# Small parameters as rows, squares shared in another order, and x turned two channel tiles at a time

## The chip, the cores and the metric

The kernel runs on one core of a Trainium2 chip. The core has a matrix engine (TensorE, PE in the profile; its weight loads are PEld), a vector engine (VectorE, DVE), a scalar engine (ScalarE, ACT), GpSimd (POOL) and a queue that starts transfers (SyncE, SP). Matrix products read SBUF, the on-chip memory of 128 partitions, and write PSUM, eight banks of 128 x 512 numbers in 32 bits. The metric is the device time of one execution in microseconds (us). The kernel before takes 730.1 us, the median of three runs (729.89 to 731.35).

## The reference

One layer of a diffusion backbone on x (512 tokens, 1024 channels), with 256 context tokens and a conditioning vector c:

```python
sh, sc, gt = split(silu(c) @ w_mod + b_mod, 3)
h = rmsnorm(x, pre_g) * (1 + sc) + sh            # and the same for the context, with c_ctx
parts = split_in(h @ w_in)                       # 10 parts of 1024 columns
q, k, v = rope(parts[4]), rope(parts[5]), parts[6]
attn = neighbourhood_attention(q, k, v, k_ctx, v_ctx, rpb)     # window 8 x 16, and all context keys
y_a = (silu(z_a) * b_gate * dwconv3(c_gate * x_in, conv_w, conv_b)) @ w_out_conv
y_b = (silu(z_b) * attn) @ w_out_attn
y = (sigmoid(g_a) * y_a + sigmoid(g_b) * y_b) @ w_o
out = x + gt * rmsnorm(y, post_g)
```

Everything is in 32-bit floating point. The change concerns the first two lines and the beginning of the third.

## The kernel before

The kernel keeps activations with channels on partitions and tokens along the free axis, in eight tiles of 128 channels (`KT` = 8). A product of near 32-bit precision is made of three products in the reduced type fp32r: each operand is split into a high part (a cast on ACT, L70) and a low part (a subtraction on DVE, L71), and high x high, high x low and low x high are added in PSUM.

The first 52 us are written in a fixed order for PE, DVE, ACT and SP (`tc.manual_schedule`, L313): on each engine the instructions stand as the program issues them. Behind it a scheduler orders the work, from its own costs.

The fixed part does the following.

1. SP loads the vector c (`crow`, L314), the four token tiles of x (`xn`, `load_x`, 128 tokens x 1024 channels each, L315), the small parameters (`sp`, L316: gains, biases and convolution weights, 72 columns), and then for each channel tile k two slabs of w_mod (`wm`, `load_slab`, L249) and one piece of the first three weight chunks (`fraw`, `load_first`, L284). All of these stand in one queue.
2. PE spreads silu(c) over all partitions (`spread`, L353, two products of one row); ACT copies the two halves into `cb` (`kept`, L357).
3. For each token tile i, `square(i)` takes the sum of squares (L333 on DVE or L337 on ACT), `root(i)` its root on ACT (L341), and `norm(i)` the reciprocal on DVE (L345) and the scaling of x: on DVE for tiles 0 to 2 (L347), on ACT for tile 3 (L349).
4. `condition(k, 0, [0])` and `condition(k, 0, [1])` make the scale and the shift of channel tile k, each a sum over 1024 products on DVE (L259). The first uses `bsc1`, a copy of a part of `sp` plus one (L375). L393 multiplies the scale by the gain.
5. PE turns x (a transpose by a product with the identity): the channel tiles 0 and 1 of all four token tiles first (L386), with products that only keep PE busy in between (`keep_busy`, L362, 128 x 256 with a result that is not used). Each such product and each spread counts as two in the profile.
6. For k = 0 to 7: ACT casts the weights (`cast_first`, L289), DVE makes the low part (`rest_first`, L293), ACT modulates the turned tile with scale and shift (L398) and casts it (L70), DVE makes its low part (L71). Then `steps(k)` makes 18 products of 128 x 512 into the six accumulators `acc` (L305, L306, L309), and behind them `turn_x(k + 2)` turns the tile that is two further (L298, four transposes). Turned tiles alternate between two PSUM banks (`tps`).

Behind this part come the convolution branch, the attention with its keys, queries and values, the gates, the merge and the output projection. PE works there almost without a gap.

Of the kernel before, what the change touches and what calls it, by code (L numbers as in the profile page):

```python
# [9 lines left out]
F32 = mybir.dt.float32  # L10
# [5 lines left out]
P = 128  # L16
# [11 lines left out]
def layer(ctx: ExitStack, tc, xp, ctxt, ctxT, cc, wmod, small, wfirst, win, wout, wo, rel, tab, out):  # L28
# [204 lines left out]
    with ExitStack() as p0:  # L233
# [3 lines left out]
        def load_x(src, i, n, tag, pool, bufs=1):  # L237
            xt = pool.tile([P, D], F32, name=n, tag=tag, bufs=bufs)
            nc.sync.dma_start(xt, src[i * P:(i + 1) * P])
            return xt  # L240
# [50 lines left out]
        def rest_first(k):  # L291
            H, L = first[k]
            nc.vector.tensor_sub(L, raws[k], H.bitcast(F32))  # L293
# [7 lines left out]
        def steps(k):  # L301
            H, L = first.pop(k)
            for i in range(6):
                cs = slice(i * P, (i + 1) * P)
                nc.tensor.matmul(acc[i], lhsT=H[:, cs], rhs=hx[0][k], start=k == 0, stop=False)  # L305
                nc.tensor.matmul(acc[i], lhsT=L[:, cs], rhs=hx[0][k], start=False, stop=False)  # L306
            for i in range(6):
                cs = slice(i * P, (i + 1) * P)
                nc.tensor.matmul(acc[i], lhsT=H[:, cs], rhs=hx[1][k], start=False, stop=k == KT - 1)  # L309
# [2 lines left out]
        E = mybir.EngineType  # L312
        with tc.manual_schedule(engines={E.PE, E.DVE, E.Activation, E.SP}):  # L313
            nc.sync.dma_start(crow, cc[0:1].rearrange("o (a n) -> o a n", a=2))  # L314
            xn = [load_x(xp, i, f"x{i}", f"u{i}", hp) for i in range(4)]  # L315
            nc.sync.dma_start(sp, small)  # L316
            for k in range(3):
                load_slab(k)
                load_first(k)

            nc.vector.memset(eps, EPS)
            nc.vector.memset(ones, 1.0)
            nc.vector.memset(allones, 1.0)

            nc.scalar.activation(crow, crow, AF.Silu)
            nc.scalar.activation(const.tile([P, 1], F32, name="dummy"), eps, AF.Sqrt)
            junk_a = hp.tile([P, D], F32, name="junka", tag="a1")

            def square(i):
                top = tops[:, i:i + 1]  # L330
                if i < 2:
                    junk = st.tile([P, D], F32, name="junk")
                    nc.vector.tensor_tensor_reduce(  # L333
                        out=junk, in0=xn[i], in1=xn[i], scale=1.0, scalar=0.0, op0=ALU.mult, op1=ALU.add, accum_out=top
                    )
                else:
                    nc.scalar.activation(junk_a, xn[i], AF.Square, accum_out=top)  # L337

            def root(i):
                top = tops[:, i:i + 1]  # L340
                nc.scalar.activation(top, top, AF.Sqrt, bias=eps, scale=1.0 / D)  # L341

            def norm(i):
                top = tops[:, i:i + 1]
                nc.vector.reciprocal(top, top)  # L345
                if i < 3:
                    nc.vector.tensor_scalar(out=xn[i], in0=xn[i], scalar1=top, scalar2=None, op0=ALU.mult)  # L347
                else:
                    nc.scalar.mul(xn[i], xn[i], top)  # L349

            def spread(i):
                ps = tps()
                nc.tensor.matmul(ps, lhsT=ones, rhs=crow[:, i], start=True, stop=True)  # L353
                return ps

            def kept(i, ps):
                nc.scalar.copy(cb[:, 0, i * S:(i + 1) * S], ps)  # L357

            def keep_busy(n):

                for _ in range(n):
                    nc.tensor.matmul(acc[5][:, :256], lhsT=ident, rhs=cb[:, 0, :256], start=True, stop=True)  # L362

            wide = [spread(i) for i in range(2)]
            square(0)
            square(1)
            kept(0, wide[0])
            root(0)
            norm(0)
            root(1)  # L370
            norm(1)
            kept(1, wide[1])
            square(2)
            root(2)
            nc.vector.tensor_scalar(out=bsc1, in0=sp[:, BM + 8:BM + 16], scalar1=1.0, scalar2=None, op0=ALU.add)  # L375
            nc.vector.tensor_scalar(out=hcv, in0=sp[:, CW:CW + 32], scalar1=0.5, scalar2=None, op0=ALU.mult)
            norm(2)
            square(3)
            root(3)
            condition(0, 0, [0])  # L380
            norm(3)
            turned_x = {k: tps() for k in range(2)}
            for t in range(4):
                keep_busy(1 if t < 2 else 2)
                for k in range(2):
                    nc.tensor.transpose(turned_x[k][:, t * P:(t + 1) * P], xn[t][:, k * P:(k + 1) * P], ident)  # L386
            keep_busy(3)

            for k in range(KT):
                cast_first(k)  # L390
                condition(k, 0, [1])
                col = cols.pop((k, 0))
                nc.vector.tensor_mul(col[:, 0:1], col[:, 0:1], sp[:, PG + k:PG + k + 1])  # L393
                rest_first(k)
                if k + 1 < KT:
                    condition(k + 1, 0, [0])
                m = st.tile([P, S], F32, name="m", bufs=2)
                nc.scalar.activation(m, turned_x.pop(k), AF.Identity, bias=col[:, 1:2], scale=col[:, 0:1])  # L398
                split(hx[0][k], hx[1][k], m)
                if k + 3 < KT:  # L400
                    load_slab(k + 3)
                    load_first(k + 3)
                elif k == 5:
                    after = Chunk(order[3])
                steps(k)
                if k + 2 < KT:
                    turned_x[k + 2] = turn_x(k + 2)
            chunk.ahead[3] = after.split()
            nc.sync.dma_start(cb[:, 1], cc[1:2].broadcast_to([P, D]))
            nc.scalar.activation(cb[:, 1], cb[:, 1], AF.Silu)  # L410
            cn = [load_x(ctxt, i, f"c{i}", f"a{2 + i}", hp) for i in range(2)]
            ctT4 = [hp.tile([P, 4, C], F32, name=f"ctT{i}", tag="a0" if i == 0 else "u3") for i in range(2)]
            for i in range(2):
                nc.sync.dma_start(ctT4[i], ctxT[:, 4 * i:4 * i + 4])
            for i in range(2):
                nc.scalar.activation(junk_a, cn[i], AF.Square, accum_out=topc[:, i:i + 1])
            nc.scalar.activation(topc, topc, AF.Sqrt, bias=eps, scale=1.0 / D)
            nc.vector.reciprocal(topc, topc)

            for i in range(2):  # L420
                nc.vector.tensor_scalar(out=diag[:, i], in0=ident, scalar1=topc[:, i:i + 1], scalar2=None, op0=ALU.mult)
# [454 lines left out]
```

## Time and profile before

| | |
|---|---|
| median of three runs | 730.1 us |
| the profiled execution | 730.62 us |
| its span, first to last instruction | 728.8 us |
| PE busy | 718.0 us (99%) |
| DVE, ACT busy | 515.1 us (71%), 331.9 us (46%) |
| step 0 begins on PE (L305) | 15.88 us |
| step 1 begins on PE | 20.52 us |

The span is counted from the first instruction; the device time has about 1.8 us around it. In the timeline a row gives the start, the length, the engine with its line, the tiles that are written and read, how often rows were joined, and in brackets how long the engine had stood idle and what released it. The length of an instruction contains its start-up and its drain, so that the next one on the same engine may start before the end that is shown.

### The profile page before, as it was taken

The numbers are of one execution on the slowest core, as the hardware profiler recorded it, in microseconds if no ns is written. First come the engines' busy times: TensorE is split into PE (matmuls) and PEld (weight loads), VectorE is DVE, ScalarE is ACT, GpSimd is POOL, SyncE is SP. The second block draws the span as 40 slices with busy tenths as digits, with TensorE's granted clock in tenths as the row PEclk, the third lists the DMA queues.
The fourth block names the chain that finished last, engine by engine and source line by source line (L and its number), as shares of the span: only waits on it lengthen the run. The fifth ranks groups of instructions, "written<-read, shape, count | busy, mean of one in ns | idle before, by whom it ended". The sixth has DMA issues, their size and how long they took to land.

```text
span 728.8 us, 9358 instructions
## 1 busy us (share of the span) xinstructions
PE 718.0 (99%) x3512; PEld 602.5 (83%) x3512; DVE 515.1 (71%) x1060; ACT 331.9 (46%) x619; POOL 0.7 (0%) x6
## 2 busy tenths in 40 slices
PE   7999999999999999999999999999999999999996
PEld 4888888888888888888888888888888888888885
DVE  6979999996998968879879779675844324335323
ACT  6565533663564654655536446434823213314221
POOL 0000000000000000000000000000000000000000
PEclk9999999999999999999999999999999999999999
DMA  8985873213212222121322212222133233235402
GB/s 334 405 310 176 317 268 125 92 65 105 65 66 73 70 76 73 58 86 59 116 73 73 73 58 73 96 78 73 58 115 102 72 116 103 71 116 177 169 10 107
DMA packets 25967, 86.63 MB, mean 119 GB/s; under 512 B 3009, under 2 KB 3393, under 8 KB 25922
## 3 DMA queue, kind: packets, MB, share of 16 engines
q1 hardware_dynamic: 25778, 85.84, 33.8%
q8 instruction: 27, 0.44, 0.2%
q10 hardware_dynamic: 144, 0.20, 0.1%
q14 instruction: 18, 0.15, 0.1%
HBM read 83.93 MB, written 2.10 MB: 118 GB/s over the span
## 4 chain that ended last, share of the span: by engine, by line
PE 95%; DVE 1%; DMA 1%; ACT 1%; SPq 0%; issue 0%; DVEq 0%; ACTq 0%
PE ps L117 20%; PE ps L116 20%; PE ps L115 20%; PE ps L128 6%; PE ps L752 6%; PE ps L597 4%; PE ps L581 4%; PE ps L132 3%; PE ps L549 3%; PE ps L140 2%; PE ps L305 2%; PE ps L309 2%; PE ps L306 2%; DMA wm<-in_wmod 1%; PE ps L558 1%; PE ps L144 1%
## 5 line engine op out<-in xcount | busy, mean ns | idle before, releaser
L115 PE MATMUL ps<-h,w 128*128 128x512 f32 x528 | 207.4, 393 | 0.0
L117 PE MATMUL ps<-h,w 128*128 128x512 f32 x528 | 206.0, 390 | 0.0
L116 PE MATMUL ps<-h,w 128*128 128x512 f32 x528 | 205.7, 390 | 0.0
L71 DVE TENSOR_TENSOR w<-raw,w 128x1024 fp32r<-128x1024 f32 (+1 forms) x98 | 113.1, 1173 | 59.0 <-ACT w L70 58.8
L70 ACT CAST w<-raw 128x1024 fp32r<-128x1024 f32 (+1 forms) x98 | 96.9, 1016 | 94.2 <-PE ps L117 64.6
L117 PEld LDWEIGHTS ps<-h,w 128*128 128x128 f32 x528 | 99.1, 188 | 20.8
L116 PEld LDWEIGHTS ps<-h,w 128*128 128x128 f32 x528 | 99.2, 188 | 20.3
L115 PEld LDWEIGHTS ps<-h,w 128*128 128x128 f32 x528 | 99.1, 188 | 20.2
L572 ACT ACTIVATE pt<-ps,m 128x512 f32<-128x512 f32 x64 | 44.3, 693 | 59.0 <-DVE m L569 59.0
L565 DVE CUSTOM_DVE_ANT_1 ps<-ps,bt 128x512 f32<-128x512 f32 x56 | 38.6, 700 | 15.1 <-PE ps L549 12.0
L71 DVE TENSOR_TENSOR TL<-ps,TH 128x512 fp32r<-128x512 f32 x64 | 42.7, 680 | 5.2 <-ACT TH L70 5.2
L128 PE MATMUL ps<-w,h 128*128 128x512 f32 x128 | 45.2, 395 | 0.0
L712 DVE SCALAR_TENSOR_TENSOR g<-g,ps 128x512 f32<-128x512 f32 x16 | 11.0, 687 | 42.5 <-PE ps L117 42.5
L70 ACT CAST TH<-ps 128x512 fp32r<-128x512 f32 x64 | 35.0, 588 | 6.6 <-PE ps L581 6.4
L630 ACT ACTIVATE g<-ps 128x512 f32<-128x512 f32 x16 | 9.6, 598 | 59.6 <-PE ps L117 59.6
L132 PE MATMUL ps<-w,h 128*128 128x256 f32 x128 | 36.0, 281 | 0.0
L581 PE MATMUL ps<-ident,pt 128*128 128x128 f32 x256 | 33.3, 272 | 0.0
L574 DVE TENSOR_SCALAR pt<-pt,z 128x512 f32<-128x512 f32 x64 | 30.8, 482 | 1.0
L581 PEld LDWEIGHTS ps<-ident,pt 128*128 128x128 f32 x256 | 29.4, 140 | 2.2
L597 PE MATMUL ps<-TH,V 128*128 128x256 f32 (+1 forms) x96 | 28.5, 319 | 0.0
L128 PEld LDWEIGHTS ps<-w,h 128*128 128x128 f32 x128 | 24.0, 187 | 5.3
L597 PE MATMUL ps<-TL,V 128*128 128x256 f32 (+1 forms) x96 | 27.7, 319 | 0.0
(158 smaller groups left out, 1183.5 us busy)
## 6 DMA issues: line engine op xcount, KB each, us to landing
raw<-in_win SPq DMA_DIRECT2D x74, 512.0 KB, 4.2
wm<-in_wmod SPq DMA_DIRECT2D x34, 512.0 KB, 6.9
raw<-in_wout SPq DMA_DIRECT2D x16, 512.0 KB, 3.9
bt<-in_rel SPq DMA_DIRECT2D x16, 256.0 KB, 2.6
raw<-in_wo SPq DMA_DIRECT2D x8, 512.0 KB, 3.7
fraw<-in_wfirst SPq DMA_DIRECT2D x8, 384.0 KB, 8.3
x<-in_xp SPq DMA_DIRECT2D x4, 512.0 KB, 5.3
xr<-in_xp SPq DMA_DIRECT2D x4, 512.0 KB, 6.2
```

Source lines behind the costliest of these rows:

```text
L70: nc.scalar.copy(H, src)
L71: nc.vector.tensor_sub(L, src, H.bitcast(F32))
L115: nc.tensor.matmul(ps, lhsT=H[:, k, cs], rhs=mH[k], start=k == 0, stop=False)
L116: nc.tensor.matmul(ps, lhsT=H[:, k, cs], rhs=mL[k], start=False, stop=False)
L117: nc.tensor.matmul(ps, lhsT=L[:, k, cs], rhs=mH[k], start=False, stop=k == KT - 1)
L128: nc.tensor.matmul(ps, lhsT=mH[k][:, ts], rhs=both[:, k].rearrange("p a c -> p (a c)"), start=k == 0, stop=False, skip_group_check=True,)
L132: nc.tensor.matmul(ps[:, :256], lhsT=mL[k][:, ts], rhs=H[:, k], start=False, stop=k == KT - 1, skip_group_check=True)
L565: nc.vector.tensor_tensor_reduce(out=s3, in0=s3, in1=bt[:, e::4 - e][:, 0:2], scale=1.0, scalar=-3.0e38, op0=ALU.add, op1=ALU.max, accum_o ...
L572: nc.scalar.activation(pt, s, AF.Exp, bias=m, scale=1.0, accum_out=z)
L581: nc.tensor.transpose(tp[:, c], pt[:, c * P:(c + 1) * P], ident)
L597: nc.tensor.matmul(o3[:, dst], lhsT=V[p][:, kt, h], rhs=src(t), start=n == 0 and t is TH, stop=n == len(work) - 1 and t is TL,)
L752: nc.tensor.matmul(ps, lhsT=mm[m][k][:, ts], rhs=w[k][:, cols], start=k + o == 0, stop=k == KT - 1 and o == 2)
```

## The change

There are three edits, all in the fixed part. The kernel's lines behind them move by four to seven numbers.

- The host passes the small parameters as 72 rows of 128 numbers in place of 128 rows of 72. They are loaded as `rows`, third in SP's queue, ahead of x2 and x3 rather than behind them. PE turns them into a PSUM bank behind the two spreads, and ACT copies the result to `sp`.
- DVE takes the squares of tiles 0 and 2, ACT those of 1 and 3 (before: DVE 0 and 1, ACT 2 and 3). The second `kept` comes ahead of the second square, and `norm(3)` ahead of the first condition sum. The small `hcv` instruction moves into the loop, behind `rest_first(0)`.
- `turn_x(k + 2)` no longer follows each step. In steps 1, 3 and 5, after six of the 18 products, two tiles are turned one after the other.

```diff
@@ steps(k)
             for i in range(6):
+                if i == 3 and k % 2 and k + 2 < KT:
+
+                    for n in (k + 1, k + 2):
+                        turned_x[n] = turn_x(n)
                 cs = slice(i * P, (i + 1) * P)
                 nc.tensor.matmul(acc[i], lhsT=H[:, cs], rhs=hx[0][k], start=k == 0, stop=False)
                 nc.tensor.matmul(acc[i], lhsT=L[:, cs], rhs=hx[0][k], start=False, stop=False)
@@ the fixed part
             nc.sync.dma_start(crow, cc[0:1].rearrange("o (a n) -> o a n", a=2))
-            xn = [load_x(xp, i, f"x{i}", f"u{i}", hp) for i in range(4)]
-            nc.sync.dma_start(sp, small)
+            xn = [load_x(xp, i, f"x{i}", f"u{i}", hp) for i in range(2)]
+            rows = st.tile([72, P], F32, name="rows")
+            nc.sync.dma_start(rows, small)
+            xn += [load_x(xp, i, f"x{i}", f"u{i}", hp) for i in range(2, 4)]
...
             def square(i):
                 top = tops[:, i:i + 1]
-                if i < 2:
+                if i % 2 == 0:
...
             wide = [spread(i) for i in range(2)]
+            nc.tensor.transpose(acc[0][:, :72], rows, ident[:72, :72])
             square(0)
-            square(1)
             kept(0, wide[0])
             root(0)
             norm(0)
+            kept(1, wide[1])
+            nc.scalar.copy(sp, acc[0][:, :72])
+            square(1)
+            square(2)
             root(1)
+            root(2)
             norm(1)
-            kept(1, wide[1])
-            square(2)
-            root(2)
             nc.vector.tensor_scalar(out=bsc1, in0=sp[:, BM + 8:BM + 16], scalar1=1.0, scalar2=None, op0=ALU.add)
-            nc.vector.tensor_scalar(out=hcv, in0=sp[:, CW:CW + 32], scalar1=0.5, scalar2=None, op0=ALU.mult)
             norm(2)
             square(3)
             root(3)
+            norm(3)
             condition(0, 0, [0])
-            norm(3)
...
                 rest_first(k)
+                if k == 0:
+                    nc.vector.tensor_scalar(out=hcv, in0=sp[:, CW:CW + 32], scalar1=0.5, scalar2=None, op0=ALU.mult)
...
                 steps(k)
-                if k + 2 < KT:
-                    turned_x[k + 2] = turn_x(k + 2)
@@ the host
     def cols(z):
-        return z.reshape(-1, 128).T
+        return z.reshape(-1, 128)
```

On DVE, in the lead-in, the row of names is: `x_120`, `x_122` and so on are the token tiles 0, 1, 2, 3 in order (in the changed kernel `x_126` is tile 2 and `x_128` tile 3), `ISA` with `junk,tops` is a square, `ISA` with `junk,col` a condition sum. Before:

```order
L345 RECIPROCAL tops<-tops 128x1 [waits Activation_49]
L347 TENSOR_SCALAR x_122<-x_122,tops 128x1024 [waits DVE_49]
L375 TENSOR_SCALAR bsc_102<-sp 128x8 [waits DMAHW5_49]
L376 TENSOR_SCALAR hcv<-sp 128x32
L345 RECIPROCAL tops<-tops 128x1 [waits Activation_49]
L347 TENSOR_SCALAR x_124<-x_124,tops 128x1024 [waits DMAHW3_49,DVE_49]
L259 ISA junk,col_178<-wm,cb,bsc_102 128x1024 [waits DMAHW6_49]
L259 ISA col_178 128x1
L345 RECIPROCAL tops<-tops 128x1 [waits Activation_49]
L259 ISA junk,col_178<-wm,cb,sp 128x1024 [waits DMAHW7_49,DVE_49]
```

And now, at the same place:

```order
L339 ISA junk,tops<-x_126 128x1024 [waits DMAHW4_49]
L339 ISA tops 128x1
L351 RECIPROCAL tops<-tops 128x1 [waits Activation_49]
L353 TENSOR_SCALAR x_122<-x_122,tops 128x1024 [waits DMAHW2_49,DVE_49]
L383 TENSOR_SCALAR bsc_102<-sp 128x8
L351 RECIPROCAL tops<-tops 128x1 [waits Activation_49]
L353 TENSOR_SCALAR x_126<-x_126,tops 128x1024 [waits DVE_49]
L351 RECIPROCAL tops<-tops 128x1 [waits Activation_49]
L259 ISA junk,col_182<-wm,cb,bsc_102 128x1024 [waits DMAHW6_49]
L259 ISA col_182 128x1
L259 ISA junk,col_182<-wm,cb,sp 128x1024 [waits DMAHW7_49,DVE_49]
```

The square of tile 2, which waits for that tile's load, stands ahead of the scaling of tile 1, and the reciprocal of tile 3 ahead of both condition sums.

On PE, the lead-in's keep-busy products and turns (`ident,x`) before:

```order
L353 MATMUL ps<-crow,ones 128x512
L362 MATMUL ps<-cb,ident 128x256 [waits Activation_49,Pool_49]
L386 MATMUL ps<-ident,x_120 128x128 [waits DVE_49]
L386 MATMUL ps<-ident,x_120 128x128 [waits Activation_49]
L362 MATMUL ps<-cb,ident 128x256
L386 MATMUL ps<-ident,x_122 128x128 [waits DVE_49]
L386 MATMUL ps<-ident,x_122 128x128
L362 MATMUL ps<-cb,ident 128x256 x2
```

And now:

```order
L359 MATMUL ps<-crow,ones 128x512
L371 MATMUL ps<-ident,rows 128x72 [waits DMAHW3_49,Pool_49]
L368 MATMUL ps<-cb,ident 128x256 [waits Activation_49]
L393 MATMUL ps<-ident,x_120 128x128 [waits DVE_49]
L393 MATMUL ps<-ident,x_120 128x128 [waits Activation_49]
L368 MATMUL ps<-cb,ident 128x256
L393 MATMUL ps<-ident,x_122 128x128 [waits DVE_49]
L393 MATMUL ps<-ident,x_122 128x128
L368 MATMUL ps<-cb,ident 128x256 x2
```

The order of turns and keep-busy products is the same; the turn of the 72 rows stands ahead of them, and what each turn waits for on DVE and ACT comes at another time.

At the end of step 0 PE had the turn of a tile ahead of step 1 (`h_81` is the modulated tile of step 1):

```order
L309 MATMUL ps<-h_80,fH 128x512 x5
L298 MATMUL ps<-ident,x_120 128x128 [waits PE_49]
L298 MATMUL ps<-ident,x_122 128x128
L298 MATMUL ps<-ident,x_124 128x128
L298 MATMUL ps<-ident,x_126 128x128
L305 MATMUL ps<-h_81,fH 128x512 [waits Activation_49]
L306 MATMUL ps<-h_81,fL 128x512 [waits DVE_49]
```

Now step 1 follows at once and has two turns inside (the first is shown):

```order
L313 MATMUL ps<-h_80,fH 128x512 x5
L309 MATMUL ps<-h_81,fH 128x512 [waits Activation_49]
L310 MATMUL ps<-h_81,fL 128x512 [waits DVE_49]
L309 MATMUL ps<-h_81,fH 128x512
L310 MATMUL ps<-h_81,fL 128x512
L309 MATMUL ps<-h_81,fH 128x512
L310 MATMUL ps<-h_81,fL 128x512
L298 MATMUL ps<-ident,x_120 128x128 [waits PE_49]
L298 MATMUL ps<-ident,x_122 128x128
L298 MATMUL ps<-ident,x_126 128x128
L298 MATMUL ps<-ident,x_128 128x128
```

Eight transposes stand behind the first six products of step 1, and nothing between the last product of step 0 and the first of step 1.

More of the change, by code (lines that the diff above doesn't have):

```diff
@@ L827, in cols @@
     def cols(z):
-        return z.reshape(-1, 128).T
+        return z.reshape(-1, 128)
     small = np.ascontiguousarray(np.concatenate(
         [cols(a["pre_g"][0]), cols(a["post_g"][0]), cols(a["b_mod"][0])]
-        + [cols(a["conv_w"][0][i]) for i in range(3)] + [cols(a["conv_b"][0])], axis=1))
+        + [cols(a["conv_w"][0][i]) for i in range(3)] + [cols(a["conv_b"][0])]))
     xp = np.ascontiguousarray(a["x"][0].reshape(ROWS, COLS, 1024).transpose(1, 0, 2)).reshape(512, 1024)
```

## The prediction

> **What bounds the kernel now.** I read the page's busy times and its chain of waits first, then the list of who waited for whom on TensorE (PE), then the timeline of the first 25 us.
>
> ```profile
> PE 718.0 (99%) x3512; PEld 602.5 (83%) x3512; DVE 515.1 (71%) x1060; ACT 331.9 (46%) x619; POOL 0.7 (0%) x6
> ...
> PE 95%; DVE 1%; DMA 1%; ACT 1%; SPq 0%; issue 0%; DVEq 0%; ACTq 0%
> ...
> PE ps L386 <- ACT x L349: 0.6, 1, 0.6
> PE ps L549 <- ACT pt L572: 0.4, 1, 0.4
> PE ps L305 <- ACT h L70: 0.3, 1, 0.3
> ```
>
> PE is the bound: 99% busy, 95% of the chain. Its waits after the opening vector are three short ones, two of them before its first real product at L305. So the change, which touches only the first 50 us, can move the end in two ways: by moving the start of step 0 (L305 of `steps(0)`), or by putting a gap into PE's work behind it. A microsecond lost or won there is one in the total.
>
> The timeline of the lead-in shows what the start of step 0 hangs on.
>
> ```profile
> 5.76 1.22 DVE L333 CUSTOM_DVE_ANT_0 junk<-x 128x1024 f32<-128x1024 f32 x1
> 5.86 0.30 ACT L341 ACTIVATE tops<-tops,eps 128x1 f32<-128x1 f32 x1
> 6.91 0.16 DVE L345 RECIPROCAL tops<-tops 128x1 f32<-128x1 f32 x1
> 7.23 0.56 ACT L357 COPY cb<-ps 128x512 f32<-128x512 f32 x1
> 7.77 0.16 DVE L345 RECIPROCAL tops<-tops 128x1 f32<-128x1 f32 x1
> 7.96 0.75 DVE L347 TENSOR_SCALAR x<-x,tops 128x1024 f32<-128x1024 f32 x1
> 8.50 1.06 ACT L337 ACTIVATE junka<-x 128x1024 f32<-128x1024 f32 x1 [0.70 <-DMA x<-in_xp]
> 9.68 0.29 ACT L341 ACTIVATE tops<-tops,eps 128x1 f32<-128x1 f32 x1
> 9.88 1.04 ACT L337 ACTIVATE junka<-x 128x1024 f32<-128x1024 f32 x1
> 10.01 0.17 DVE L375 TENSOR_SCALAR bsc<-sp 128x8 f32<-128x8 f32 x1 [1.30 <-DMA sp<-in_small]
> 10.09 0.18 DVE L376 TENSOR_SCALAR hcv<-sp 128x32 f32<-128x32 f32 x1
> 11.05 0.29 ACT L341 ACTIVATE tops<-tops,eps 128x1 f32<-128x1 f32 x1
> 11.22 1.28 DVE L259 CUSTOM_DVE_ANT_0 junk<-wm,cb,bsc 128x1024 f32<-128x1024 f32 x1
> 12.43 0.16 DVE L345 RECIPROCAL tops<-tops 128x1 f32<-128x1 f32 x1
> 12.61 1.28 DVE L259 CUSTOM_DVE_ANT_0 junk<-wm,cb,sp 128x1024 f32<-128x1024 f32 x1
> 12.62 1.15 ACT L349 ACTIVATE x<-x,tops 128x1024 f32<-128x1024 f32 x1 [1.28 <-DVE tops L345]
> 13.68 0.82 ACT L289 CAST fH<-fraw 128x768 fp32r<-128x768 f32 x1
> 13.82 0.15 DVE L393 TENSOR_TENSOR col<-col,sp 128x1 f32<-128x1 f32 x1
> 14.40 0.77 ACT L398 ACTIVATE m<-ps,col 128x512 f32<-128x512 f32 x1
> 15.88 0.51 PE L305 MATMUL ps<-h,fH 128*128 128x512 f32 x1 [0.31 <-ACT h L70]
> ```
>
> Three things are to be seen. x2 came at 8.50, late against x1 (whose square began at 5.76). The wait for `sp` at 10.01 looks like the target, but the first condition sum behind it (11.22) waits for its own slab. And the modulation at 14.40 follows the cast on ScalarE (ACT), not DVE, whose column was made at 13.82.
>
> **The change, part by part.** *Small parameters as rows.* The transfer stands third instead of fifth in SP's queue, so x2 and x3 wait behind it and the slabs do not. Its price: x3 was in use at 9.88 and `sp`, queued behind it, at 10.01, so 0 to 0.3 us; I take 0.15. x2 is then usable at 8.65, x3 at 10.03 or before. PE's turn of 72 rows stands behind the two spreads, in time that PE does not need. The copy out of PSUM on ACT lies between the 0.30 us of a 128x1 and the 0.56 us of a 128x512 row: 0.3 us, behind the second `kept`, which cannot start before 7.05 (the end of the spreads, below). Queued behind the copy is the square of x1.
>
> *Squares.* ACT now squares x1 from about 8.0, and its root starts 1.18 us later (8.50 to 9.68), done by 9.5. DVE squares x2 from 8.65 and takes the reciprocal of x1 1.15 us later (5.76 to 6.91), at 9.80. Reciprocal and scaling take 0.86 us to the next instruction (6.91 to 7.77): `bsc1` at 10.66, 0.08 later (10.01 to 10.09) x2's reciprocal at 10.74, x3's at 11.60. On ACT the root of x2 starts at about 9.92, the square of x3 0.20 later (9.68 to 9.88), its root 1.17 after that (9.88 to 11.05) at 11.29, done 11.58: just in time. Then the two condition sums. `norm(3)` now stands ahead of the first, so this sum waits for x3's whole chain: it starts 0.19 after 11.60, at 11.79, not at 11.22. The second follows 1.3 us later and the column 1.21 us after that (12.61 to 13.82), at 14.33.
>
> ACT is eased: it scales x3 at 11.8 instead of 12.62. But `fH` needs its load, for which the row says only that it had come by 13.68, so the cast frees ACT by 14.40 at the latest. The column reaches ACT 0.25 us after its start (rows below, 18.41 to 18.66), so the modulation starts at 14.58 instead of 14.40. From there to step 0 it is 1.48 us as before (14.40 to 15.88): **16.06, that is +0.18**.
>
> *Turns.* The rows around the end of step 0:
>
> ```profile
> 18.41 0.15 DVE L393 TENSOR_TENSOR col<-col,sp 128x1 f32<-128x1 f32 x1
> 18.66 0.78 ACT L398 ACTIVATE m<-ps,col 128x512 f32<-128x512 f32 x1 [0.81 <-DVE col L393]
> 18.77 1.56 PE L309 MATMUL ps<-h,fH 128*128 128x512 f32 x6
> 19.47 0.62 ACT L70 CAST h<-m 128x512 fp32r<-128x512 f32 x1
> 20.16 0.60 PE L298 MATMUL ps<-ident,x 128*128 128x128 f32 x4
> 24.78 0.60 PE L298 MATMUL ps<-ident,x 128*128 128x128 f32 x4
> ```
>
> A step with its turn takes 24.78 - 20.16 = 4.62 us. In the row of six, the starts of products are (1.56 - 0.39)/5 = 0.23 us apart, so 18 products are 4.18 and four turns 0.44. Six tiles turned one by one or in pairs are 24 instructions either way: 2.64 us, no difference. What is lost is a cover: the turn behind step 0 hid that `h` of step 1 is ready only at 19.47 + 0.62 = 20.09, made at DVE's pace. DVE's work behind the column stays as dense (the `hcv` instruction of 0.09 us moves to between 15.3 and 15.4, where DVE had stood idle before), so 20.09 stays. PE leaves step 0 at 16.06 + 4.18 = 20.24, so the uncovered wait costs nothing; but it means that a start before 15.9 would no longer be worth anything. Later turns end before the modulation that reads them is due: tile 2 by about 22.1 against 22.6. Tiles 4 and 6 come out some 1 to 1.5 us later than before, within step 3 and 5, but their `h` still stands more than 1 us ahead of its step. Cost nothing; if that lead were gone, about 1 us each.
>
> Behind step 7 the order is a scheduler's, and it comes out nearly as before: on PE one small product moves back by three, on ACT and DVE some neighbours change places until about 125 us. PE waits there for 0.4 us in all (L549, above), so the loads and casts have room to shift; cost nothing.
>
> *PE's lead-in.* This is the part that is easily missed. Between the turns of x stand products that only keep PE busy (L362).
>
> ```profile
> 3.27 3.78 PE L353 MATMUL ps<-crow,ones 1*128 1x512 f32 x4 [3.27 <-ACT crow L325]
> 6.98 1.22 PE L362 MATMUL ps<-cb,ident 128*128 128x256 f32 x2
> 8.42 1.06 PE L362 MATMUL ps<-cb,ident 128*128 128x256 f32 x2
> 9.70 1.91 PE L362 MATMUL ps<-cb,ident 128*128 128x256 f32 x4
> 11.41 0.64 PE L386 MATMUL ps<-ident,x 128*128 128x128 f32 x2
> 11.84 1.36 PE L362 MATMUL ps<-cb,ident 128*128 128x256 f32 x4
> 14.10 1.46 PE L362 MATMUL ps<-cb,ident 128*128 128x256 f32 x6
> ```
>
> From 9.70 to 11.41 four of them are 0.43 us apart; six from 14.10 are (1.46 - 0.38)/5 = 0.22 apart. PE's pace doubles within the row of 11.84, at 12 to 13 us, after 5.0 to 6.0 us of almost unbroken work from 6.98 on. In the changed kernel the turn of x1 has to wait for its scaling, which now stands behind the square of x2: 10.66 + 0.1, against 8.7 before. PE runs out of work at about 9.4 and stands until about 10.85, and everything behind is in order on its queue: the turns of x1, x2 and x3 (0.43 us each at the slow pace) and seven keep-busy calls (0.85 each, two products), 7.27 us in all. At the slow pace this lasts until 18.1, past 16.06; if the pace doubles at time w, until (18.1 + w)/2. It reaches 16.06 only if w is 14.0 or less.
>
> No row shows w after a break of 1.4 us. Lower bound: the break does not count, w stays at 12.5, cost 0. Upper bound by the nearest row: the count starts again at 10.85 and takes about 5.5 us, w = 16.4, lead-in until 17.25, cost +1.2. I take the middle, **+0.6**, since the row that I have is one sample of when the pace turned, not of what it needs.
>
> [...]
>
> **Sum.** +0.18 for the chain, 0 for the turns, +0.6 for the lead-in: +0.8 us. Against the profiled execution (730.62, span 728.8) that is 731.4; this execution stands 0.5 above the median of the runs, 730.1, which I use: **730.9 us**. The forecast's own range is +0.2 to +1.4, 730.3 to 731.5. About 0.2% (1.5 us) is what a measurement of this kernel can tell from no change, so this is most likely none.
>
> **Rivals.** *Slower: the pace turns too late.* If the first work that counts was the spread at 3.27 (row L353), the pace took about 9 us to turn, w is near 20 here, the whole lead-in runs slow until 18.1 (+2.0) and four or five products of step 0 take 0.43 instead of 0.23 (+0.9): 732.3 with the lead-in alone, 733.2 with both. It decides once w is beyond 16.6 (the lead-in then ends at 17.35, 1.5 behind the old start). For it: the spreads did not speed up in 3.6 us of their own. Against: they use one row of the array (1x512), so they may not count.
>
> *The lead-in does not matter.* w stays below 14.0: only the chain's +0.18 is left, 730.3. For it: the break is 1.4 us, and the stop from 13.2 to 13.8 did not undo the pace before. Against: that stop came after the pace had turned.
>
> *Faster: x2 comes early.* x2 took 2.7 us behind x1, x3 only 1.4 behind x2. If the extra 1.3 us was an accident of this execution, DVE's square of x2 starts at 7.3; then x1's root (9.5, on ACT) binds, DVE runs 0.33 earlier than in my sum and the lead-in as well: about -0.2, 729.9. More is not to be had, since step 1 then stands on DVE's pace. Against: the old order would win as much or more from an early x2, since its condition sum waits for a slab alone.
>
> **How the numbers follow.** The forecast (+0.2 to +1.4) has 0.55, the late pace 0.17, the lead-in that does not matter 0.16, the early x2 0.12. Slower by over 0.2% (above 731.6): the late pace and 0.05 from the forecast's upper end, 0.22. Faster by over 0.2% (below 728.6): no sum reaches it; half of the early x2, for a load stream that is early as a whole, 0.06. Within: 0.72. The range goes from 729.5 (below the early x2) to 732.4 (the late pace by its lead-in alone).
>
> **What would show it.** In the changed profile the first condition sum should start near 11.8, the column near 14.3, `h` of step 0 near 15.4; PE should stand still from about 9.4 to 10.9, its keep-busy products should still be 0.43 us apart after 13, and step 0 should wait for the last of them rather than for `h`. A pair of turns in step 1 should take 0.88 us with no wait in front of step 1. I am wrong if the keep-busy products are at 0.22 before 14, if step 0 starts before 15.9, or if PE waits for `h` in front of steps 1 to 7.

## The result, and the profile after

The changed kernel takes 731.73 us (median of 21 runs, 730.85 to 732.77), the kernel before 730.40 in the runs beside it (21 runs, 729.87 to 731.35). The ratio is 1.0018, with a 95% interval of 1.0011 to 1.0024: slower by 1.33 us, just inside the bound of 0.2%. Predicted were 730.9 us and a range of 729.5 to 732.4.

Each run of the changed kernel lists its span beside its time, so the loss can be split. For the kernel before, such a list is on record for the 33 runs beside the first four experiments (median 730.47 us), and these are used. The median span went from 728.7 to 729.6 us, **0.9 us inside the program**. What lies around the span (time minus span, run by run) went from 1.79 (1.75 to 1.83) to 2.13 us (2.07 to 2.17), **0.34 us outside it**. The profiled execution (731.27 us, span 729.1) is one of the shorter ones: its span is only 0.3 above the 728.8 of the profile before, and its rows show less than the median's loss.

The page after, with the busy times and the chain:

```profile
span 729.1 us, 9362 instructions
PE 718.2 (98%) x3513; PEld 603.0 (83%) x3513; DVE 515.0 (71%) x1060; ACT 332.2 (46%) x620; POOL 0.7 (0%) x6
...
PE 96%; DVE 1%; DMA 1%; ACT 1%; issue 0%; SPq 0%; DVEq 0%; ACTq 0%
```

PE is the bound as before. The list of PE's waits after (total, times, longest, in us):

```profile
PE ps L359 <- ACT crow L331: 3.3, 1, 3.3
PE ps L393 <- DVE x L353: 0.9, 1, 0.9
PE ps L556 <- ACT pt L579: 0.4, 1, 0.4
```

The wait for x3's scaling on ACT (0.6) has gone, and the one for `h` ahead of step 0 (0.3) has shrunk until the list no longer names it. One for x1's scaling on DVE has come, 0.9 us. The timeline after, around the lead-in:

```profile
8.37 1.23 DVE L339 CUSTOM_DVE_ANT_0 junk<-x 128x1024 f32<-128x1024 f32 x1 [1.23 <-DMA x<-in_xp]
8.52 1.06 PE L368 MATMUL ps<-cb,ident 128*128 128x256 f32 x2
9.71 0.76 DVE L353 TENSOR_SCALAR x<-x,tops 128x1024 f32<-128x1024 f32 x1
10.53 0.69 PE L393 MATMUL ps<-ident,x 128*128 128x128 f32 x2 [0.95 <-DVE x L353]
11.00 1.91 PE L368 MATMUL ps<-cb,ident 128*128 128x256 f32 x4
11.41 1.27 DVE L259 CUSTOM_DVE_ANT_0 junk<-wm,cb,bsc 128x1024 f32<-128x1024 f32 x1
12.71 0.63 PE L393 MATMUL ps<-ident,x 128*128 128x128 f32 x2
13.14 1.36 PE L368 MATMUL ps<-cb,ident 128*128 128x256 f32 x4
13.93 0.16 DVE L400 TENSOR_TENSOR col<-col,sp 128x1 f32<-128x1 f32 x1
14.33 0.38 PE L393 MATMUL ps<-ident,x 128*128 128x128 f32 x2
14.55 1.46 PE L368 MATMUL ps<-cb,ident 128*128 128x256 f32 x6
14.64 0.78 ACT L407 ACTIVATE m<-ps,col 128x512 f32<-128x512 f32 x1 [0.63 <-PE ps L393]
15.45 0.62 ACT L70 CAST h<-m 128x512 fp32r<-128x512 f32 x1
16.12 0.50 PE L309 MATMUL ps<-h,fH 128*128 128x512 f32 x1
20.40 0.39 PE L309 MATMUL ps<-h,fH 128*128 128x512 f32 x1
21.80 1.04 PE L298 MATMUL ps<-ident,x 128*128 128x128 f32 x8
25.46 0.40 PE L309 MATMUL ps<-h,fH 128*128 128x512 f32 x1
```

DVE squares x2 at 8.37 and scales x1 only at 9.71, so PE stands until 10.53. From there the order on PE holds: turn, keep-busy products, turn. The pace is still slow at 11.00 (0.43 us from product to product, 1.71 for four). It doubles within the row of 13.14: its four products take 1.19 us to the next row, which is 1.5 of them at 0.43 and 2.5 at 0.22, so at about 13.8 us; before, the same count gives 12.5. (Products are counted here as the profile does, two for each matrix product that `keep_busy` issues.) The column of step 0 is ready at 14.1, but ACT's modulation at 14.64 had stood 0.63 us for PE, for the last turn at 14.33. Step 0 begins at 16.12 (before 15.88), step 2 at 25.46 (before 25.13).

Step 0 still follows `h` and not the end of PE's queue: the last keep-busy product had ended at 16.01 (14.55 + 1.46), the cast of `h` ended at 16.07 (15.45 + 0.62). In ten of the kernels traced here the rows show the modulation, and step 0 begins 1.47 to 1.48 us behind its start; eight of them also show the cast, and step 0 begins 0.05 to 0.06 us behind its end. So the late turn of x1 reaches step 0 through the turn of x3 and the modulation that reads it.

The delay at step 2 is the measure of what the lead-in costs, since nothing behind takes it back: span minus the start of step 2 is 703.6 us after (729.1 - 25.46) and 703.7 before (728.8 - 25.13).

### The profile page after: what moved, and what is told of

It is laid out like the page before. It is cut to its first block, busy times and chain, and to the rows that moved or that the text cites. A ratio compares the mean times of both kernels' runs of the same rounds, so it can differ in the third digit from the quotient of the medians.

```text
span 729.1 us, 9362 instructions
## 1 busy us (share of the span) xinstructions
PE 718.2 (98%) x3513; PEld 603.0 (83%) x3513; DVE 515.0 (71%) x1060; ACT 332.2 (46%) x620; POOL 0.7 (0%) x6
## 4 chain that ended last, share of the span: by engine, by line
PE 96%; DVE 1%; DMA 1%; ACT 1%; issue 0%; SPq 0%; DVEq 0%; ACTq 0%
PE ps L117 20%; PE ps L115 20%; PE ps L116 20%; PE ps L128 6%; PE ps L759 6%; PE ps L604 4%; PE ps L588 4%; PE ps L132 3%; PE ps L556 3%; PE ps L140 2%; PE ps L309 2%; PE ps L310 2%; PE ps L313 2%; PE ps L565 1%; PE ps L144 1%; DMA x<-in_xp 1%
## 5 line engine op out<-in xcount | busy, mean ns | idle before, releaser
L521 ACT ACTIVATE qd<-ta 64x512 fp32r<-64x512 f32 x32 | 20.2, 631 | 24.0 <-DVE ta L495 15.8
```

## The experiments

**The edits one by one.** First each edit alone on the kernel before: the pairs of turns, the 72 rows, and the other order of the squares (with `kept` and `norm(3)` at their new places; `hcv` stays where it was).

```diff
@@ the turns alone
+                if i == 3 and k % 2 and k + 2 < KT:
+                    for n in (k + 1, k + 2):
+                        turned_x[n] = turn_x(n)
...
-                if k + 2 < KT:
-                    turned_x[k + 2] = turn_x(k + 2)
@@ the rows alone (the order of loads and the host as in the change)
+            nc.tensor.transpose(acc[0][:, :72], rows, ident[:72, :72])
...
+            nc.scalar.copy(sp, acc[0][:, :72])
@@ the squares alone
-                if i < 2:
+                if i % 2 == 0:
...
             square(0)
-            square(1)
             kept(0, wide[0])
             root(0)
             norm(0)
+            kept(1, wide[1])
+            square(1)
+            square(2)
             root(1)
+            root(2)
             norm(1)
-            kept(1, wide[1])
-            square(2)
-            root(2)
...
+            norm(3)
             condition(0, 0, [0])
-            norm(3)
```

> The kernel before with one of the three edits alone: two tiles of x are turned inside steps 1, 3 and 5. Before: 730.4 us; the changed kernel: 731.7. Theory of the lead-in (the loss is that PE's keep-busy products start anew late, behind the late turn of token tile 1, and run at the slow pace): nothing of that is in this kernel, so 730.4, within 0.2; step 0 starts at 15.9 and step 1 at 20.1 to 20.2. Rival of the turns (the uncovered wait in front of step 1, or turned tiles that come too late for steps 4 and 6): up to the whole loss, 731.0 to 731.7, with PE waiting for h in front of a step.

> The kernel before with one edit alone: the small parameters as 72 rows, third in the queue of loads, turned by PE and copied by ACT. Theory of the lead-in: the squares of tiles 0 and 1 stay on DVE, tile 1 is scaled by 8.8 us and PE's lead-in has no break, so 730.4, within 0.2. Rival of the loads (x2 and x3 come later behind the rows, and all that follows is late): 0.2 to 0.4 more, 730.6 to 730.8, with x2's square on ACT starting at 8.7 or later.

> The kernel before with one edit alone: DVE squares token tiles 0 and 2, ACT 1 and 3, and the reciprocal of tile 3 stands ahead of the first condition sum; small parameters and turns as before. Theory of the lead-in: tile 1 is scaled only after the square of tile 2, at about 10.5 us, PE stands for about 1 us before it turns tile 1, its pace doubles at 13.8 us or later, and nearly the whole loss is here: 731.2 to 731.8. Rival of the vector chain alone (the condition sum waits for tile 3's reciprocal): 730.5 to 730.7, the sums starting 0.2 to 0.6 us later, with PE's pace without part in it.

Beside a kernel before of 730.47 us, the medians of 11 runs each:

| | time | ratio (95%) | median span | around it |
|---|---|---|---|---|
| turns alone | 730.47 | 0.9999 (0.9990 to 1.0007) | 728.7 | 1.77 |
| rows alone | 730.54 | 1.0007 (0.9998 to 1.0016) | 728.8 | 1.78 |
| squares alone | 731.17 | 1.0009 (1.0000 to 1.0018) | 729.1 | 2.13 |

Turns and rows cost nothing that can be told from noise; three of the eleven runs with the rows alone lie 0.8 to 1.9 us above their median, and no run shows why. The squares bring the whole 0.34 around the span, and 0.4 of the 0.9 within it; their time of 731.17 stands at the low end of the 731.2 to 731.8 expected, so it isn't nearly the whole loss. Their timeline shows the same gap and late pace as the whole change:

```profile
7.18 1.23 DVE L333 CUSTOM_DVE_ANT_0 junk<-x 128x1024 f32<-128x1024 f32 x1
...
9.11 0.16 DVE L345 RECIPROCAL tops<-tops 128x1 f32<-128x1 f32 x1 [0.70 <-ACT tops L341]
...
10.12 0.69 PE L386 MATMUL ps<-ident,x 128*128 128x128 f32 x2 [0.61 <-DVE x L347]
...
12.74 1.79 PE L362 MATMUL ps<-cb,ident 128*128 128x256 f32 x4
...
13.60 0.15 DVE L393 TENSOR_TENSOR col<-col,sp 128x1 f32<-128x1 f32 x1
...
14.37 0.38 PE L386 MATMUL ps<-ident,x 128*128 128x128 f32 x2
...
14.68 0.78 ACT L398 ACTIVATE m<-ps,col 128x512 f32<-128x512 f32 x1 [1.61 <-PE ps L386]
```

The column was made at 13.60, earlier than in the kernel before (13.82), and ACT stood 1.61 us for PE's turn of x3. So it is not the vector chain that is late. One thing differs from the changed kernel: here x2 had come early (its square on DVE begins at 7.18 rather than 8.37), and x1's reciprocal waited for x1's own root on ACT, whose square had moved there. The gap is then 0.61 us instead of 0.95. So either move can hold x1 back: the square of x2 ahead of its scaling on DVE, or its own square on ACT. Whether x2 comes later in most executions of the whole change, and the span loses 0.9 rather than 0.4 for that reason, no run shows.

The complement, the whole change without the squares (squares, `norm(3)` and `hcv` as before):

> The changed kernel without its middle edit: rows and turns as changed, squares and their order as before. Theory of the lead-in: no break, so no loss, and the rows let step 0 begin at 15.4 to 15.9: 730.2 to 730.5, and 1.8 us around the span. Rival, that two edits harm only together (the uncovered wait in front of step 1 with late loads): 730.8 or more, with PE waiting for h in front of step 1.

It took 730.47 us (11 runs) beside 730.33, ratio 1.0000 (0.9991 to 1.0008), span 728.7, around it 1.79. The loss comes with the squares' edit and goes with it. The other two edits, harmless alone and together, do not explain why the span loses twice as much with them as with the squares alone; that stays open.

**Is it PE's gap?** In the changed kernel one more keep-busy product and one of half its width (four in the profile's count, about 1.3 us at the slow pace) were put ahead of the turn of x1, so that PE has work while DVE is busy with x2. The vector chain stays as in the change.

```diff
             for t in range(4):
                 keep_busy(1 if t < 2 else 2)
+                if t == 1:
+                    keep_busy(1)
+                    nc.tensor.matmul(acc[5][:, :128], lhsT=ident, rhs=cb[:, 0, :128], start=True, stop=True)
```

> The changed kernel, but PE's break of about 1 us before the turn of token tile 1 is filled with one and a half more keep-busy products (their result is not used). Theory of the lead-in: PE's work is unbroken from 7 us on, its pace doubles by 13.8 us at the latest, the turn of tile 3 is no longer late and the loss falls from 1.3 us to what the vector chain costs, 0.2 to 0.4: 730.6 to 730.8, and the runs lie closer together than the 1.9 us between the lowest and the highest of the changed kernel. Rivals that put the loss elsewhere (vector chain, loads, turns): 731.7 as before, or a little more, since PE has more to do.

Measured: 730.79 us (11 runs), span 728.7, around it 2.14; the ratio to the kernel before is 1.0006 (0.9997 to 1.0015). The span is that of the kernel before again, although PE has more to do and the chain is unchanged. PE's busy time by stretches of 1 us, first after (the changed kernel), then filled (columns: stretch, its length, PE busy with the count, clock, DMA share, GB/s):

```profile
9.00:10.00 1.00, 0.58 (x2) 1.00 1.03 414
10.00:11.00 1.00, 0.47 (x2) 1.00 1.01 413
```

```profile
9.00:10.00 1.00, 1.00 (x4) 1.00 1.02 418
10.00:11.00 1.00, 1.00 (x5) 1.00 1.02 419
```

And the timeline of the filled kernel:

```profile
8.51 1.91 PE L368 MATMUL ps<-cb,ident 128*128 128x256 f32 x4
...
11.07 1.56 PE L368 MATMUL ps<-cb,ident 128*128 128x256 f32 x4
...
12.69 1.03 PE L368 MATMUL ps<-cb,ident 128*128 128x256 f32 x4
...
13.55 0.38 PE L396 MATMUL ps<-ident,x 128*128 128x128 f32 x2
...
14.16 0.78 ACT L410 ACTIVATE m<-ps,col 128x512 f32<-128x512 f32 x1 [0.15 <-DVE col L403]
...
15.64 0.50 PE L309 MATMUL ps<-h,fH 128*128 128x512 f32 x1 [0.41 <-ACT h L70]
```

Without the gap the four products from 12.69 are already at 0.22 us each ((1.03 - 0.38)/3), x3 is turned at 13.55 rather than 14.33, and the modulation waits for DVE's column instead of for PE. PE waits for `h` again ahead of step 0, which begins at 15.64. So the loss within the span is the gap ahead of the turn of x1, with what it does to PE's pace and, through both, to the turn of x3.

**Is it the vector chain?** My +0.18 rested on `norm(3)` standing ahead of the first condition sum. It was put behind it, the rest as in the change.

```diff
-            norm(3)
             condition(0, 0, [0])
+            norm(3)
```

> The changed kernel with one line moved back: the reciprocal of token tile 3 stands behind the first condition sum again. Theory of the lead-in: token tile 1 is still scaled behind the square of tile 2, so PE still has its break and its late pace; the reciprocal of tile 3 comes 1.2 us later, its scaling ends at 13.9 instead of 12.7, which the slow lead-in hides: span 729.4 to 729.8 as in the changed kernel. Rival of the vector chain (the loss comes from the condition sum that waits for tile 3's reciprocal): the sums start 0.1 to 0.3 us earlier and the span falls to that of the kernel before, 728.6 to 728.8.

Measured: 731.45 us (11 runs) beside 730.33, ratio 1.0017 (1.0008 to 1.0026), span 729.4, around it 2.02. Nothing was won. The timeline:

```profile
10.42 0.69 PE L393 MATMUL ps<-ident,x 128*128 128x128 f32 x2 [0.77 <-DVE x L353]
...
14.74 0.61 PE L393 MATMUL ps<-ident,x 128*128 128x128 f32 x2
15.17 1.48 PE L368 MATMUL ps<-cb,ident 128*128 128x256 f32 x6
16.68 0.50 PE L309 MATMUL ps<-h,fH 128*128 128x512 f32 x1
...
15.20 0.78 ACT L407 ACTIVATE m<-ps,col 128x512 f32<-128x512 f32 x1 [0.72 <-PE ps L393]
```

In this execution the pace doubled only at about 15.2: the two transposes of 14.74 still take 0.43 us, the six products behind them are 0.22 apart ((1.48 - 0.38)/5). Step 0 begins at 16.68, 0.56 later than in the profile of the change, and the span is 729.7 rather than 729.1. Two executions with nearly the same gap (0.77 and 0.95 us), the pace 1.4 us later in one, and a span longer by 0.6: that is nearly the half of the shift, as when slow products become fast ones.

**Are the keep-busy products worth their time?** In the changed kernel they were left out, all of them; their results are not used.

> The changed kernel without any keep-busy product (their results are not used in the changed kernel either). Theory of the lead-in: the turn of tile 3 is no longer late and step 0 starts at about 15.7, 0.4 us earlier than in the changed kernel's profile, but its products run at the slow pace (0.43 us apart) for 3 to 7 us, until PE has worked long enough: 1.5 to 3.4 us lost there, 732.3 to 734.2. Rival, that the pace turns with time and not with work (13.8 us): step 0 starts at 15.7 at the full pace, 730.8.

It took 733.17 us (4 runs), ratio 1.0036 (1.0023 to 1.0050), span 731.05. The timeline:

```profile
13.47 0.69 PE L392 MATMUL ps<-ident,x 128*128 128x128 f32 x2 [0.59 <-ACT x L355]
16.40 0.80 PE L309 MATMUL ps<-h,fH 128*128 128x512 f32 x1 [2.25 <-ACT h L70]
17.00 0.63 PE L310 MATMUL ps<-h,fL 128*128 128x512 f32 x1
17.42 0.63 PE L309 MATMUL ps<-h,fH 128*128 128x512 f32 x1
17.85 0.63 PE L310 MATMUL ps<-h,fL 128*128 128x512 f32 x1
```

PE stood 2.25 us for `h`, and then the real products run 0.43 us apart. How long they do so, 3 to 7 us in the expectation, was an estimate; the rows show it as far as 17.85. Step 0 did not start at the 15.7 expected: in this execution x2 was in use only at 9.10 (8.37 in the profile of the change), so how much earlier step 0 could start without the keep-busy products isn't shown. What they save shows in the median span, 731.05 us without them and 729.6 with them.

**What lies around the span.** The busy instructions of DVE are 1060 before and after, but the trace has 1209 records of DVE before and 1207 after (the page doesn't count those that only wait or set semaphores). To see whether the number matters, two clears of 128x1 were put at the start of DVE's program, where it stands idle.

```diff
             nc.vector.memset(allones, 1.0)
+            for i in range(2):
+                nc.vector.memset(const.tile([P, 1], F32, name=f"spare{i}"), 0.0)
```

> The changed kernel with two more small clears on DVE (128x1, never read) at about 1.2 us, where DVE has nothing to do. Every run of the changed kernel, of the squares alone and of the filled lead-in has a device time 2.1 us above its span; every run of the kernel before, of the turns alone and of the rows alone 1.8 us. The DVE programs of the first three have two records fewer in the trace (waits) than those of the others. Theory that the time around the span goes with the length of DVE's program: back to 1.8, device time 731.4, the span as in the changed kernel (729.6). Rival, something else of the squares edit, or of the program as a whole: 2.1 stays, 731.7.

The changed kernel with them took 730.94 us (11 runs) beside 730.33, with 1.80 us around the span, as before the change. Its median span was 729.2. Its lead-in was no better (in the profile the turn of x1 waited 1.52 us and step 0 began at 16.95), so the smaller span was not explained. The next runs show why. Two of them are the kernel before with two and with four such clears, and one is the filled kernel with two.

> The kernel before with two spare clears of 128x1 on VectorE at the start. If the time around the span falls steadily with the number of VectorE instructions (2.13 at 1207 records, 1.79 at 1209), it is about 1.45 us here at 1211. If it has two levels only, it stays at 1.8 or goes back to 2.1. The span stays at 728.7 in each case.

> The kernel before with four spare clears of 128x1 on VectorE at the start (1213 records). Falling steadily: about 1.1 us around the span. Two levels: 1.8 or 2.1. Whatever comes out, together with the run of two clears it shows whether the number of instructions has a direction or only a pattern. The span stays at 728.7.

> The changed kernel with both additions: three more keep-busy products in TensorE's gap before the turn of x1 (as in the filled kernel) and two spare clears of 128x1 on VectorE at the start. If the loss has two parts that add, 0.9 us in the span from TensorE's lead-in and 0.34 us around the span from VectorE's program, both are gone: span 728.7, around it 1.80, time 730.5, equal to the kernel before. If the clears of the run before acted only because something else in that run was different, the time around the span stays at 2.13 and the time at 730.8.

The last one is the filled kernel with two more instructions that clear no tiles of their own:

```diff
             nc.vector.memset(allones, 1.0)
+            for i in range(2):
+                nc.vector.memset(eps, EPS)
```

> The filled kernel with two more VectorE instructions as in the run before it, but they clear no tiles of their own: they write the tile eps a second and third time with the same value, so nothing is allocated and no address of another tile moves. If the number of VectorE's instructions sets the time around the span, it is 1.80 us again, not 2.14; if the two spare tiles did it by moving addresses, it stays at 2.14. The same for the 0.65 us that the kernels with spare tiles win in the span between 150 and 525 us, in steps of a few ns over the products: if the instructions did it, the time from the 145th product of the steps to the end of the span is 676.1 us and the span 727.8; if the addresses did it, 676.8 us and a span of 728.5.

All with the median of their own runs (10 or 11 each, 21 for the changed kernel, 33 for the kernel before), in the order of DVE's records. They were measured in several groups. The kernel before had 730.33 us and a median span of 728.5 beside the kernels with spare tiles and the one with `norm(3)` back, 730.50 and 728.7 beside the one with `eps` written again:

| | DVE records | time | around the span | median span |
|---|---|---|---|---|
| changed, `norm(3)` back | 1206 | 731.45 | 2.02 | 729.4 |
| changed | 1207 | 731.73 | 2.13 | 729.6 |
| filled | 1207 | 730.79 | 2.14 | 728.7 |
| before | 1209 | 730.47 | 1.79 | 728.7 |
| changed, two clears of spare tiles | 1209 | 730.94 | 1.80 | 729.2 |
| filled, two clears of spare tiles | 1209 | 729.59 | 1.77 | 727.8 |
| filled, `eps` written again twice | 1209 | 730.54 | 1.78 | 728.8 |
| before, two clears of spare tiles | 1211 | 729.93 | 1.97 (1.73 to 2.11) | 728.0 |
| before, four clears of spare tiles | 1213 | 730.05 | 2.13 | 727.9 |

Two things follow. The time around the span goes with DVE's program: two more instructions, whatever they write, take the filled kernel from 2.14 to 1.78. But it has no direction: 1.8 at 1209, 2.13 at 1207 and at 1213 again. The steady fall that one expectation named is wrong. What happens in that time isn't visible, since nothing of it lies in the trace.

The second effect came unasked: wherever spare tiles were added, the median span fell by 0.4 to 1.0 us (by 0.5 and 0.6 against the kernel before in its own group), and writing `eps` again did not do that. The timelines of the filled kernel, of the one with `eps` written again, and of the one with spare tiles, in this order: the start of step 2, and the first product of the same later group (`us` as its stationary side).

```profile
25.00 0.40 PE L309 MATMUL ps<-h,fH 128*128 128x512 f32 x1
...
525.18 0.39 PE L115 MATMUL ps<-us,w 128*128 128x512 f32 x1
```

```profile
24.73 0.40 PE L309 MATMUL ps<-h,fH 128*128 128x512 f32 x1
...
524.89 0.39 PE L115 MATMUL ps<-us,w 128*128 128x512 f32 x1
```

```profile
24.81 0.40 PE L309 MATMUL ps<-h,fH 128*128 128x512 f32 x1
...
524.35 0.39 PE L115 MATMUL ps<-us,w 128*128 128x512 f32 x1
```

Between the two rows lie 500.18, 500.16 and 499.54 us. With the spare tiles the same products, in the same order, take 0.6 us less there. In the kernel before and the changed one, also without spare tiles, the same stretch takes 500.26 us (25.13 to 525.39) and 500.21 (25.46 to 525.67). From the start of step 2 to the end of the span it is 703.0, 703.1 and 703.2 us in three traces with spare tiles (the filled kernel, and the kernel before with two and with four), and 703.6 to 703.7 in the four without (before, changed, filled, `eps` written again). In the profiles of the filled kernels 1963 products fall between 150 and 525 us with the spare tiles, 1961 and 1960 without. That the spare tiles do it is shown. That they do it by moving the tiles behind them to other addresses is the reading I hold likely, but no run here varied an address alone.

The filled kernel with spare tiles takes 729.59 us (729.44 to 730.73), 2.1 us less than the changed kernel. Against the kernel before it is 0.9992 (0.9983 to 1.0000): at the edge of what can be told.

## Why the prediction was right or wrong

The time was 0.8 us above the forecast of 730.9: within the whole range, above the forecast's own 730.3 to 731.5. About 0.3 of the 0.8 is the base, since the kernel before took 730.40 beside the changed one and not 730.1. The change itself, +1.33, lies within the +0.2 to +1.4, but partly by luck: a term of 0.18 was nothing, and one of 0.34 was missing. Step by step:

- **Turns, 0 us:** right. Alone they measure 0.9999. Step 1 with its pair takes 25.46 - 20.40 = 5.06 us, which is 4.18 + 0.88 as worked out. The lost cover cost nothing, and PE waits for no `h` between the steps.
- **Rows, 0.15 us on x2 and the copy of 0.3:** this term did not matter. x2 was in use at 8.37 (before 8.50), the copy took 0.22, and alone the edit measures 1.0007 with an interval that holds 1.
- **The chain, +0.18:** this step failed. The first condition sum was to start at 11.79 and the column at 14.33; they came at 11.41 and 13.93. More than that, the column is not what the modulation of step 0 waits for. I had `h` depend on column and ACT, and PE's lead-in act only as a queue ahead of step 0. But the modulation reads the turned tile, whose last piece is the turn of x3, and that stands in PE's queue behind the keep-busy products. The row of 14.64 shows it (0.63 us for PE), and so does the kernel with `norm(3)` back, where nothing was won. The term is 0. That the modulation came when forecast (14.64, forecast 14.58) is luck: the column was 0.4 us early, and the turn of x3 held it.
- **The lead-in, +0.6 (0 to +1.2):** the cause was right, the path to step 0 wrong, and the size too small. PE's stop came as foreseen (9.6 to 10.5, forecast 9.4 to 10.9), and the pace doubled late, at 13.8 in the profile of the change and at about 15.2 in that with `norm(3)` back. But the forecast had step 0 wait for the last keep-busy product rather than for `h`, and it waits for `h`. By the forecast's own formula a doubling at 13.8 ends the lead-in at (18.1 + 13.8)/2 = 15.95, ahead of its 16.06, and costs nothing; step 0 came at 16.12 all the same, by way of the turn of x3. Only with the doubling at 15.2 did the queue end no earlier than `h`: the last keep-busy product ended at 16.65, the cast of `h` at 16.63. By the median span the lead-in costs 0.9, and filling the gap takes it all back.
- **The working:** two sums in it are loose, 10.66 + 0.1 taken as 10.85 and 11.79 + 1.3 + 1.21 as 14.33. Both are within 0.1 us, and nothing hangs on them.
- **Around the span, 0 in my sum:** this is the missing term, 0.34 us. I carried the 1.8 us over from the profile before as if they were a constant. With it the sum of measured terms is 0 + 0 + 0.9 + 0.34 = 1.24, of the 1.33 between the medians (1.26 against the 730.47 of the runs that the spans are from).

Of the rivals, the late pace (doubling near 20 us) did not come: the latest doubling with keep-busy products is that at 15.2. Without any of them the products were still 0.43 us apart at 17.85. "The lead-in does not matter" falls with the filled kernel. Of the early x2, x2 came 0.13 us earlier than before, and the gap was there nonetheless; in the kernel with the squares alone it came early indeed, x1's own root on ACT bound, as that rival said, and step 0 began no earlier (16.16). My test "wrong if the keep-busy products are at 0.22 before 14" was too sharp: they are from 13.8 on, in this one execution.

When PE's pace doubles was measured here, and is not explained. In seven lead-ins without a gap, which start alike at 7.0 to 7.2, it doubled anywhere between 10.2 and 12.5 us (12.5 in the kernel before, 11.3 with the turns alone, 10.2 in the filled kernel with spare tiles), that is 3.0 to 5.5 us after the start. Behind a gap it doubled at 13.8, 14.3, 14.8 and 15.2, which is 3.3 to 4.8 us after the turn that ended it. Whether the work ahead of a gap counts in part no run shows. The forecast's +0.6 for the lead-in, the middle of 0 and +1.2, was an estimate from one row; the measured +0.9 in the span lies in the upper half.

## What to carry to other kernels

A queue of products that only keep PE busy is a chain like any other: whatever real work stands behind them in order, here the turns of x, comes late when one operand ahead is late (the turn of x3 at 14.33 us, against 13.55 with the gap filled), and the pace turned later as well (at 13.8 to 15.2 behind a gap, at 10.2 to 12.5 without). So when the work of DVE or ACT is put in another order, follow each operand to the place in PE's queue where it is read, and refill the gap that it leaves. Under a microsecond, look also at what lies outside the span, and try a change of the same size that has nothing to do with the edit, before a difference is put down to the edit.

## What was not expected of the hardware

- The time around the span depends on the number of instructions in DVE's program, between 1.77 and 2.14 us, in no steady direction (1207, 1209, 1211, 1213 records: 2.13, 1.79, 1.97, 2.13). Its mechanism is open.
- Two unused tiles of 128x1 made a later stretch of 500 us in the filled kernel shorter by 0.6 us (499.54 against 500.18 and 500.16), with the order of the work unchanged.
- The clock column of the profile can't be used in this lead-in. It shows 1.00 where the keep-busy products are still 0.43 us apart (the stretches from 9 to 11 us above), and 1.00 as well from 14 to 15 us, where they are 0.22 apart. In these two traces the first record of the clock starts at 13.79 us (the changed kernel) and at 12.50 (the kernel before), where the distance of the products puts the doubling, at 13.8 and 12.5.
